# Taking an unread store out of a hybrid-attention kernel and giving two projections other PSUM banks

## Chip, core and metric

The kernel runs on one core of one Trainium2 chip. The metric is device time in microseconds (us) of one execution; smaller is better. The change is judged against the median of three runs of the kernel before.

## What is computed

One decoder block on a sequence of 1024 tokens with 1024 channels: a normalisation, one wide input projection, native sparse attention beside an RWKV-7 recurrence, a gated merge, and a convolutional feed-forward network. Only the first part of it is touched by the change:

```python
h = _rms_norm(x, norm_mix[l])
u = h @ w_in[l]
q, kc, vc, ks, vs, kw, vw, nsa_gl, rw, merge = _split(u, IN_SPLITS)
# in the attention:
qh    = _rms_norm(q.reshape(B, S, G, HG, Dh), qk_gain[0])   # four pairs of heads
k_slc = _rms_norm(ks ..., qk_gain[2])                       # "selected" keys
k_win = _rms_norm(kw ..., qk_gain[3])                       # "local" (window) keys
```

The normalised input `h` is used by every column of `u`, and nowhere else.

## The kernel before, in words

The data lie transposed: 8 chunks of 128 channels, each with 1024 tokens, cut into two halves of 512 tokens (`H[0]`, `H[1]`). Products are made exact enough by splitting each operand into a high part (`hhi`, `whi`) and a rest (`hlo`, `wlo`): `mm3` issues 24 matmuls for one output of 128 by 512, first eight times (hi times hi, lo times hi), then eight times hi times `wlo`.

**Normalisation.** For each half, ScalarE squares the eight chunks, TensorE sums them (L291), ScalarE makes `rstd`. Then `normed` goes through the eight chunks: VectorE writes `hf` (L205), a DMA of the SyncE queue stores it to `h_d` (L207), ScalarE copies it to `hhi` (L208), and VectorE, or GpSimd for chunks 1, 4 and 7 (`NPOOL`), writes `hlo` (L209). `hf` has three buffers, so the fourth chunk writes over the first one's. `hprep`, which would read `h_d`, is in no list of work.

**First projections.** `kphase` projects compressed keys and values (`W01`, banks P and B), adds a position term on VectorE (L349, tile `zpe`, which needs the load `pe`), runs 64 small matmuls per matrix (L357), projects the natural-order columns (L393, banks A), and then the selected keys (`"s"`) and local keys (`"w"`) in `project` with the default banks P. Each half of `s`, `w` and of a query pair goes through `rms64` out of its PSUM bank: square on ScalarE (`nsq`, L297), a matmul into a bank M (L299), Ln and Exp on ScalarE (L301, L302), and the product on VectorE that reads the bank for the last time (L303, `kn` or `qn`). `qproj(0)` is the first query pair; the attention itself begins after it.

**Banks.** PSUM has eight banks of 128 by 512, handed out in pairs by tag:

```python
banks = {"P": [0, 1], "M": [2, 3], "A": [4, 5], "B": [6, 7]}
```

In the attention A and B hold scores and outputs, M the maxima and the sums of `rms64`. P also belongs to the fillers: the projections of the recurrence (`zproj`), of the merge gates (`mproj`) and a low-rank stage (`loraproj`, L827), whose twelve outputs per half go through three `zs` buffers to DRAM.

**Order.** Each engine runs its own instructions in a fixed order. That order is made when the program is built: a planner simulates the program with its own costs, takes what is ready, lowest priority number first, and the fillers have numbers 10000 above the attention. All loads and stores are issued by SyncE, in one order. Weights are loaded by `wload` through two buffers of each of `wraw`, `whi` and `wlo`; ScalarE makes `whi` (L218), GpSimd `wlo` (L219).

Of the kernel before, what the change touches and what calls it, by code (L numbers as in the profile page):

```python
# [7 lines left out]
F32 = mybir.dt.float32  # L8
# [9 lines left out]
S = 1024  # L18
# [113 lines left out]
def build(tc, D, dbg=None, upto=99):  # L132
    nc = tc.nc
    V, A, G, T = nc.vector, nc.scalar, nc.gpsimd, nc.tensor
    dbg = dbg or {}

    def load(t, src):
        return nc.sync.dma_start(t, src)

    with ExitStack() as ctx:  # L140
        def pool(name, bufs=1, space=None, stack=ctx, **kw):
            if space is not None:
                kw["space"] = space
            return stack.enter_context(tc.tile_pool(name=name, bufs=bufs, **kw))
# [4 lines left out]
        dr = pool("dram", 1, DRAM)  # L149
# [7 lines left out]
        def P(name, j=0):  # L157
            o = PAR[name][0]
            return par[:, o + j:o + j + 1]
# [16 lines left out]
        def ps(tag):  # L176
            b = banks[tag]
            b.append(b.pop(0))
            return pp.tile([128, 512], F32, name="ps" + tag, tag=f"bank{b[-1]}", bufs=1)
# [5 lines left out]
        hhi, hlo = [None, None], [None, None]  # L185
# [7 lines left out]
        H = [slice(0, 512), slice(512, 1024)]  # L193

        def rstd_of(h, pss, rstd):
            A.activation(rstd[:, H[h]], pss, AF.Ln, bias=epst[:, 0:1], scale=1.0 / 1024)
            A.activation(rstd[:, H[h]], rstd[:, H[h]], AF.Exp, scale=-0.5)

        def ks_(t, k):
            return t[k] if isinstance(t, list) else t[:, k]  # L200

        def normed(h, xs, gname, rstd, hi, lo, tmp, save=None):
            for k in range(8):
                hf = tmp.tile([128, 512], F32, name="hf", bufs=3)
                V.scalar_tensor_tensor(hf, xs[k][:, H[h]], P(gname, k), rstd[:, H[h]], op0=ALU.mult, op1=ALU.mult)  # L205
                if save is not None:
                    nc.sync.dma_start(save[k][:, H[h]], hf)  # L207
                A.activation(ks_(hi[h], k), hf, AF.Copy)  # L208
                (G if k in NPOOL else V).tensor_sub(ks_(lo[h], k), hf, ks_(hi[h], k).bitcast(F32))  # L209

# [2 lines left out]
        def wload(src, nk):  # L213
            hi = wp.tile([128, 8, 128], FR, name="whi", bufs=2)
            lo = wp.tile([128, 8, 128], FR, name="wlo", bufs=2)
            raw = wp.tile([128, 8, 128], F32, name="wraw", bufs=2)[:, :nk]
            lastw[0] = load(raw, src).ins
            A.activation(hi[:, :nk], raw, AF.Copy)  # L218
            G.tensor_sub(lo[:, :nk], raw, hi[:, :nk].bitcast(F32))  # L219
            return hi, lo  # L220

        def mm3(ps, whi, wlo, xhi, xlo, nk):
            n = 0
            for k, a, b in [(k, whi, b) for k in range(nk) for b in (xhi, xlo)] + [(k, wlo, xhi) for k in range(nk)]:
                T.matmul(ps, a[:, k], ks_(b, k), start=(n == 0), stop=(n == 3 * nk - 1))  # L225
                n += 1

        def project(src, xhi, xlo, nk, evac, halves=(0, 1), tag="P"):
            hi, lo = src if isinstance(src, tuple) else wload(src, nk)
            for h in halves:  # L230
                pj = ps(tag)
                mm3(pj, hi, lo, xhi[h], xlo[h], nk)
                evac(h, pj)

        h_d = dr.tile([8, 128, S], F32, name="h_d")
        onsa_d = dr.tile([4, 128, S], F32, name="onsa_d")
        orw_d = [dr.tile([4, 128, 512], F32, name=f"orw_d{h}") for h in range(2)]
        sg_d = dr.tile([16, 128, S], F32, name="sg_d")
# [38 lines left out]
        with ExitStack() as st:  # L277
            xp = pool("x", 1, stack=st)
            W01 = []
            xs = [xp.tile([128, S], F32, name=f"x{k}") for k in range(8)]  # L280
            for h in range(2):
                for k in range(8):
                    load(xs[k][:, H[h]], D["xT"][k][:, H[h]])
                W01.append(wload(D["w_t"][h], 8))
            rstd = xp.tile([128, S], F32, name="rstd")
            for h in range(2):
                pss = ps("M")
                for k in range(8):
                    sq = xp.tile([128, 512], F32, name="sq", bufs=3)
                    A.activation(sq, xs[k][:, H[h]], AF.Square)  # L290
                    T.matmul(pss, ones, sq, start=(k == 0), stop=(k == 7))  # L291
                rstd_of(h, pss, rstd)
                normed(h, xs, "norm_mix", rstd, hhi, hlo, xp, h_d)

        def rms64(px, n, gcol, out, tmp):
            sq = tmp.tile([128, 512], F32, name="nsq", tag="nsq", bufs=2)
            A.activation(sq[:, :n], px, AF.Square)  # L297
            pss = ps(RTAG)
            T.matmul(pss[:, :n], blk, sq[:, :n], start=True, stop=True)  # L299
            rs = tmp.tile([128, 512], F32, name="nrs", bufs=2)  # L300
            A.activation(rs[:, :n], pss[:, :n], AF.Ln, bias=epst[:, 0:1], scale=1.0 / 64)  # L301
            A.activation(rs[:, :n], rs[:, :n], AF.Exp, scale=-0.5)  # L302
            V.scalar_tensor_tensor(out, px, gcol, rs[:, :n], op0=ALU.mult, op1=ALU.mult)  # L303

        WT = D["w_t"]
# [6 lines left out]
        def kstack(nm, br, kh, kl):  # L312
            n = kh.shape[1]
            so = PAR["sel"][0] + br
            for g in range(2):
                own = slice(64 * g, 64 * g + 64)
                oth = slice(64 - 64 * g, 128 - 64 * g)
                nc.sync.dma_start(kst1[nm, g][own], kh[own])
                nc.sync.dma_start(kst1[nm, g][oth], kl[own])
                nc.sync.dma_start(kst2[nm, g][own], kh[own])  # L320
                V.tensor_copy(kst2[nm, g][oth], par[oth, so:so + 1].to_broadcast([64, n]))

        def kphase():
            with ExitStack() as st:
                tmp = pool("ktmp", 1, stack=st)
# [16 lines left out]
                for kv in range(2):  # L342
# [4 lines left out]
                    def ev(h, pj):  # L347
                        for j in range(2):
                            V.tensor_tensor(z[:, j, 32 * h:32 * h + 32], pj.rearrange("p (n l) -> p n l", l=16),  # L349
                                            pe[:, kv, 16 * j:16 * j + 16][:, None, :].to_broadcast([128, 32, 16]),  # L350
                                            op=ALU.add)
# [53 lines left out]
                for nm, br, wi, gi in (("s", 0, 2, 2), ("w", 1, 3, 3)):  # L405
                    kh = tmp.tile([128, S], F16, name="kh")
                    kl = tmp.tile([128, S], F16, name="kl")

                    def ev(h, pj):
                        kn = tmp.tile([128, 512], F32, name="kn", bufs=2)  # L410
                        rms64(pj, 512, P("gain", gi), kn, tmp)
                        A.activation(kh[:, H[h]], kn, AF.Copy)
                        V.tensor_sub(kl[:, H[h]], kn, kh[:, H[h]])

                    project(WT[wi], hhi, hlo, 8, ev)
                    kstack(nm, br, kh, kl)
                    yield KY[2 + br]

# [3 lines left out]
        qpair = {}  # L422
        mark = {}

        def qproj(i):
            qh = AQ["p"].tile([128, S], F16, name="qh", bufs=2)
            ql = AQ["p"].tile([128, S], F16, name="ql", bufs=2)

            def ev(h, pj):
                qn = AQ["p"].tile([128, 512], F32, name="qn", tag="nsq", bufs=2)  # L430
                rms64(pj, 512, P("gain", 0), qn, AQ["p"])
                if 'qn' in dbg:
                    nc.sync.dma_start(dbg['qn'][i][:, H[h]], qn)
                A.activation(qh[:, H[h]], qn, AF.Copy)
                V.tensor_sub(ql[:, H[h]], qn, qh[:, H[h]])

            project(WT[4 + i], hhi, hlo, 8, ev)
            qpair[i] = (qh, ql)

        def attention():  # L440
            yield from kphase()
            AQ["p"] = pool("attq", 1, stack=ast)
            for i in range(2):
                m = AQ["p"].tile([128, 8, 64], F16, name=f"Mt{i}")
                G.memset(m, 0.0)
                Mt.append(m)
            qproj(0)
            yield KY[4]
            for i in range(4):
                qh, ql = qpair.pop(i)  # L450
# [157 lines left out]
        def reload(src):  # L608
            hi, lo = ktiles(FP["h"], "hhi"), ktiles(FP["h"], "hlo")
            for k in range(8):  # L610
                t = FP["f"].tile([128, 512], F32, name="zs", bufs=NZS)
                load(t, src(k))
                A.activation(hi[k], t, AF.Copy)
                V.tensor_sub(lo[k], t, hi[k].bitcast(F32))
            return hi, lo

        def hprep(h):
            hhi[h], hlo[h] = reload(lambda k: h_d[k][:, H[h]])

        def nsaprep():  # L620
            nsa["hi"], nsa["lo"] = reload(lambda k: onsa_d[k % 4][:, H[k // 4]])
# [605 lines left out]
        with ExitStack() as st:  # L1227
            tp_ = pool("rt", 1, stack=st)
            rstd = tp_.tile([128, S], F32, name="rstd")
# [23 lines left out]
        for g0 in range(0, 22, GR):  # L1253
            ks = range(g0, min(22, g0 + GR))
            hd_, wd_ = [], []
            for i in ks:
                uv = []
                for o in range(2):
                    ci = 22 * o + i
                    hi, lo = wload(D["f_up"][ci], 8)  # L1260
# [71 lines left out]
```

## Time and profile before

| | us |
|---|---|
| median of three runs (lowest, highest) | 1910.56 (1908.12, 1914.51) |
| the profiled execution | 1910.36 |
| its span, first to last instruction | 1908.6 |
| TensorE (PE) busy in the span | 1838.6 |
| VectorE (DVE) busy | 974.3 |
| mean granted TensorE clock (1 is full speed) | 0.98 |

In the rows of the profile PE is TensorE's matmuls, PEld its weight loads, DVE VectorE, ACT ScalarE, POOL GpSimd and SPq SyncE's queue of DMA issues; L205 is line 205 of the kernel. A row of a timeline gives the start and the duration in us, the engine, line and operation, out<-in, and in brackets how long the engine was idle before it and what ended that.

### The profile page before, as it was taken

Reading aid. Unit: us, or ns where it says so; the run is one execution under the profiler, and the core shown is the slowest. Engines: PE = TensorE matmul, PEld = TensorE weight load, DVE = VectorE, ACT = ScalarE, POOL = GpSimd, SP = SyncE. Lnnn points to the kernel's source line nnn. Section 1 sums busy time; section 2 is a strip of 40 time slices with the busy share of each in tenths; the row PEclk is TensorE's granted clock in tenths of the full one; section 3 lists DMA queues with packets and bytes.
Section 4 is the critical chain, followed back from the end, with each engine's and each line's share of the span. In section 5 each row is a group of like instructions: output and inputs, shape, how many; then the busy total and the mean of one; then the engine's idle time right before and its main releaser. Section 6 shows DMA issues by size and latency. Waiting matters only on the chain.

```text
span 1908.6 us, 30508 instructions
## 1 busy us (share of the span) xinstructions
PE 1838.6 (96%) x12106; PEld 1421.8 (74%) x12106; DVE 974.3 (51%) x1775; ACT 794.4 (42%) x1432; POOL 655.6 (34%) x412
## 2 busy tenths in 40 slices
PE   7999999999999999999999799999999999999998
PEld 4876557676767778778777578778888888888886
DVE  4313556777676411984444444355566653444444
ACT  4333565656655632455555443344222222222220
POOL 4312123122333334211245444756444433213220
PEclk9999899999999999899999899999999999999999
DMA  7414234132333435354553454426222211111102
GB/s 247 133 39 144 73 116 133 49 120 62 108 130 115 143 124 201 127 167 156 173 176 118 154 160 141 164 93 215 83 88 78 89 61 56 44 34 58 42 12 88
DMA packets 123647, 215.42 MB, mean 113 GB/s; under 512 B 23921, under 2 KB 52977, under 8 KB 123249
## 3 DMA queue, kind: packets, MB, share of 16 engines
q1 hardware_dynamic: 123504, 213.48, 33.9%
q8 instruction: 95, 1.56, 0.3%
q14 instruction: 48, 0.39, 0.1%
HBM read 151.00 MB, written 57.67 MB: 109 GB/s over the span
## 4 chain that ended last, share of the span: by engine, by line
PE 44%; DVE 2%; DMA 2%; issue 2%; ACT 1%; POOL 0%; SPq 0%; POOLq 0%; ACTq 0%
PE psA L225 11%; PE psP L225 9%; PE psM L225 9%; PE psP L1307 6%; PE psB L1307 6%; DMA s<-sg_d 1%; DVE hf L205 1%; PE psA L1084 1%; PE psM L1003 0%; DVE fu L723 0%; DMA draw<-f_dn 0%; DMA zs<-orw_d 0%; PE psC L1137 0%; DVE yl L677 0%; PE psC L1142 0%
## 5 line engine op out<-in xcount | busy, mean ns | idle before, releaser
L219 POOL TENSOR_TENSOR wlo<-wraw,whi 128x1024 fp32r<-128x1024 f32 (+1 forms) x154 | 346.5, 2251 | 589.2 <-ACT whi L218 174.8
L225 PE MATMUL psP<-hhi,whi 128*128 128x512 f32 x848 | 350.4, 414 | 22.8 <-ACT hhi L708 8.1
L225 PE MATMUL psP<-hlo,whi 128*128 128x512 f32 x848 | 345.7, 408 | 3.6 <-DVE hlo L709 2.4
L218 ACT ACTIVATE whi<-wraw 128x1024 fp32r<-128x1024 f32 (+1 forms) x154 | 152.4, 990 | 222.6 <-PE psP L225 97.9
L225 PE MATMUL psP<-hhi,wlo 128*128 128x512 f32 x848 | 224.6, 399 | 0.0
L225 PEld LDWEIGHTS psP<-hhi,whi 128*128 128x128 f32 x848 | 164.4, 194 | 65.5 <-ACT hhi L708 9.9
L225 PEld LDWEIGHTS psP<-hlo,whi 128*128 128x128 f32 x848 | 164.3, 194 | 42.7 <-DVE hlo L709 3.7
L225 PEld LDWEIGHTS psP<-hhi,wlo 128*128 128x128 f32 x848 | 158.2, 189 | 35.1 <-issue 1.2
L542 DVE TENSOR_TENSOR pl<-pf,ph 128x512 f16<-128x512 f32 (+4 forms) x208 | 122.8, 598 | 45.5 <-ACT pf L541 44.7
L540 ACT ACTIVATE ph<-psA 128x512 f16<-128x512 f32 (+4 forms) x208 | 98.8, 475 | 84.2 <-PE psA L535 60.7
L484 DVE TENSOR_REDUCE mp<-psM 128x1 f32<-128x512 f32 (+1 forms) x192 | 94.1, 515 | 47.6 <-PE psM L482 39.4
L1294 POOL TENSOR_TENSOR dl<-draw,dh 128x1024 fp32r<-128x1024 f32 x22 | 53.2, 2434 | 156.1 <-ACT dh L1293 96.9
L541 ACT ACTIVATE pf<-psA 128x512 f32<-128x512 f32 (+4 forms) x208 | 99.3, 477 | 0.0
L1271 DVE SCALAR_TENSOR_TENSOR u<-psA,par,u 128x511 f32<-128x511 f32 x64 | 47.7, 746 | 100.8 <-ACT u L1267 100.4
L1309 DVE TENSOR_TENSOR x<-x,psP 128x512 f32<-128x512 f32 x88 | 60.3, 685 | 69.1 <-PE psP L1307 68.7
L1293 ACT ACTIVATE dh<-draw 128x1024 fp32r<-128x1024 f32 x22 | 22.3, 1053 | 152.4 <-PE psB L1307 148.2
L1309 DVE TENSOR_TENSOR x<-x,psB 128x512 f32<-128x512 f32 x88 | 60.3, 685 | 45.2 <-PE psB L1307 45.2
L1271 DVE SCALAR_TENSOR_TENSOR u<-psM,par,u 128x511 f32<-128x511 f32 x64 | 47.8, 746 | 64.8 <-ACT u L1267 64.4
L1288 POOL TENSOR_TENSOR hl<-th,hh 128x1024 fp32r<-128x1024 f32 x22 | 52.9, 2402 | 74.6 <-ACT hh L1287 74.6
L545 PEld LDWEIGHTS <-ph 128*128 128x128 f16 (+1 forms) x592 | 55.8, 96 | 23.5 <-issue 10.8
L550 PEld LDWEIGHTS <-pl 128*128 128x128 f16 (+1 forms) x592 | 55.2, 98 | 22.5 <-DVE pl L542 7.9
L1307 PE MATMUL psP<-hh,dh 128*128 128x512 f32 x176 | 69.0, 392 | 2.1 <-ACT hh L1287 2.1
(374 smaller groups left out, 4204.7 us busy)
## 6 DMA issues: line engine op xcount, KB each, us to landing
wraw<-f_up SPq DMA_DIRECT2D x68, 512.0 KB, 3.3
wraw<-w_t SPq DMA_DIRECT2D x46, 512.0 KB, 3.6
draw<-f_dn SPq DMA_DIRECT2D x22, 512.0 KB, 3.2
sg_d<-zs SPq DMA_DIRECT2D x32, 256.0 KB, 2.0
wraw<-w_out SPq DMA_DIRECT2D x16, 512.0 KB, 3.4
z_d<-zs SPq DMA_DIRECT2D x28, 256.0 KB, 2.2
x<-xT SPq DMA_DIRECT2D x24, 256.0 KB, 5.9
zs<-sg_d SPq DMA_DIRECT2D x24, 256.0 KB, 3.0
```

The source lines that it names most:

```text
L218: A.activation(hi[:, :nk], raw, AF.Copy)
L219: G.tensor_sub(lo[:, :nk], raw, hi[:, :nk].bitcast(F32))
L225: T.matmul(ps, a[:, k], ks_(b, k), start=(n == 0), stop=(n == 3 * nk - 1))
L484: V.reduce_max(mp[:, x, br, t:t + 1], pm[:, 0:(b1 - b0) * 128], axis=AX.X)
L540: A.activation(ph[0:nkey, rg], pa[0:nkey, rg], AF.Exp, scale=0.125)
L541: A.activation(pf[0:nkey, rg], pa[0:nkey, rg], AF.Exp, scale=0.125)
L542: V.tensor_sub(pl[0:nkey, rg], pf[0:nkey, rg], ph[0:nkey, rg])
L545: T.matmul(pov[:, t, :], ph[0:nkey, tk], vt[0:nkey, kb, g, 0:65], start=first, stop=False, skip_group_check=True)
L550: T.matmul(pov[:, t, :], pl[0:nkey, tk], vt[0:nkey, kb, g, 0:65], start=False, stop=True, skip_group_check=True)
L1271: V.scalar_tensor_tensor(u[:, e0 + d:e0 + 512], pj[:, 0:512 - d], cw_, u[:, e0 + d:e0 + 512], op0=ALU.mult, op1=ALU.add)
L1307: T.matmul(pj, a[:, m], b[:, H[h]], start=(n == 0), stop=(n == 3 * len(hd_) - 1))
L1309: V.tensor_add(x2[m][:, H[h]], x2[m][:, H[h]], pj)
```

## The change

The store of `hf` to `h_d`, the tensor `h_d`, and the function that would have read it are gone. The local keys' projection writes banks B in place of P, and that of the first query pair banks A in place of P. The other query pairs stay in P.

```diff
-        def normed(h, xs, gname, rstd, hi, lo, tmp, save=None):
+        def normed(h, xs, gname, rstd, hi, lo, tmp):
             for k in range(8):
                 hf = tmp.tile([128, 512], F32, name="hf", bufs=3)
                 V.scalar_tensor_tensor(hf, xs[k][:, H[h]], P(gname, k), rstd[:, H[h]], op0=ALU.mult, op1=ALU.mult)
-                if save is not None:
-                    nc.sync.dma_start(save[k][:, H[h]], hf)
                 A.activation(ks_(hi[h], k), hf, AF.Copy)
...
-        h_d = dr.tile([8, 128, S], F32, name="h_d")
...
-                normed(h, xs, "norm_mix", rstd, hhi, hlo, xp, h_d)
+                normed(h, xs, "norm_mix", rstd, hhi, hlo, xp)
...
-                    project(WT[wi], hhi, hlo, 8, ev)
+                    project(WT[wi], hhi, hlo, 8, ev, tag="PB"[br])
...
-        def qproj(i):
+        def qproj(i, tag="P"):
...
-            project(WT[4 + i], hhi, hlo, 8, ev)
+            project(WT[4 + i], hhi, hlo, 8, ev, tag=tag)
...
-            qproj(0)
+            qproj(0, "A")
...
-        def hprep(h):
-            hhi[h], hlo[h] = reload(lambda k: h_d[k][:, H[h]])
```

`br` is 0 for the selected keys (banks P as before) and 1 for the local keys (banks B).

## Rows read from the trace of the kernel before

**Rows 1.** The page: the span, the busy time of each engine (us, share of the span, instructions), and the granted TensorE clock in 40 slices of 47.7 us, in tenths.
```profile
span 1908.6 us, 30508 instructions
PE 1838.6 (96%) x12106; PEld 1421.8 (74%) x12106; DVE 974.3 (51%) x1775; ACT 794.4 (42%) x1432; POOL 655.6 (34%) x412
PEclk9999899999999999899999899999999999999999
```

**Rows 2.** The page: the chain of work that ended last, by engine.
```profile
PE 44%; DVE 2%; DMA 2%; issue 2%; ACT 1%; POOL 0%; SPq 0%; POOLq 0%; ACTq 0%
```

**Rows 3.** Stretches of the span (from and to, us): length, then busy us (instructions) of PE, PEld, DVE, ACT and POOL, then the granted TensorE clock, the DMA share and GB/s.
```profile
20.00:30.00 10.00, 8.36 (x29) 4.96 (x28) 5.10 (x7) 5.59 (x10) 5.33 (x3) 1.00 0.55 155
30.00:40.00 10.00, 5.70 (x16) 4.13 (x15) 2.88 (x5) 1.26 (x2) 1.28 (x1) 0.69 0.81 281
...
55.47:126.68 71.21, 71.21 (x455) 63.46 (x453) 16.31 (x38) 19.34 (x47) 14.77 (x6) 1.00 0.29 88
...
130.00:140.00 10.00, 8.07 (x25) 5.34 (x24) 1.05 (x2) 4.11 (x7) 3.38 (x5) 0.84 0.42 95
...
180.00:190.00 10.00, 7.85 (x26) 2.65 (x25) 4.27 (x10) 2.52 (x4) 3.66 (x6) 0.87 0.74 235
190.00:200.00 10.00, 10.00 (x25) 3.28 (x25) 2.47 (x5) 3.25 (x5) 2.00 (x3) 0.50 0.48 184
200.00:210.00 10.00, 10.00 (x40) 5.89 (x39) 1.03 (x5) 2.59 (x5) 2.15 (x4) 0.77 0.38 134
```

**Rows 4.** What DVE waited for between 17 and 56 us: us in total, times, longest.
```profile
DVE hf L205 <- DMA h_d<-hf: 11.6, 6, 4.0
...
DVE zpe L349 <- DMA pe<-pe: 3.8, 1, 3.8
DVE hlo L209 <- ACT hhi L208: 1.6, 2, 0.9
```

**Rows 5.** The lines of `normed` between 17.6 and 55.4 us, each from the view of its own line: count, duration in ns (least, median, most), first and last start; the last row is the landing of the 16 stores.
```profile
L205 DVE SCALAR_TENSOR_TENSOR hf<-x,par,rstd x16: 737/748/1489, 17.6 to 48.4; 128x512 f32<-128x512 f32 x16
...
L209 DVE TENSOR_TENSOR hlo<-hf,hhi x10: 678/686/983, 19.7 to 49.0; 128x512 fp32r<-128x512 f32 x10
L209 POOL TENSOR_TENSOR hlo<-hf,hhi x6: 1277/1470/1671, 20.3 to 49.9; 128x512 fp32r<-128x512 f32 x6
...
DMA to landing us min/median/max: 2.0/2.8/7.4
```

**Rows 6.** Timelines of DVE and of POOL, in the first normalisation and, from 1282 us on, in the second one, which stores nothing.
```profile
17.65 2.08 DVE L205 SCALAR_TENSOR_TENSOR hf<-x,par,rstd 128x512 f32<-128x512 f32 x3 [9.40 <-ACT rstd L197]
22.28 2.39 POOL L219 TENSOR_TENSOR wlo<-wraw,whi 128x1024 fp32r<-128x1024 f32 x1 [0.71 <-ACT whi L218]
...
41.38 1.67 POOL L209 TENSOR_TENSOR hlo<-hf,hhi 128x512 fp32r<-128x512 f32 x1 [4.38 <-ACT hhi L208]
42.11 1.49 DVE L205 SCALAR_TENSOR_TENSOR hf<-x,par,rstd 128x512 f32<-128x512 f32 x1 [0.22 <-DMA h_d<-hf]
...
49.87 1.29 POOL L209 TENSOR_TENSOR hlo<-hf,hhi 128x512 fp32r<-128x512 f32 x1 [2.59 <-ACT hhi L208]
...
1282.89 2.76 POOL L219 TENSOR_TENSOR wlo<-wraw,whi 128x1024 fp32r<-128x1024 f32 x1 [3.23 <-ACT whi L218]
1283.32 2.88 DVE L205 SCALAR_TENSOR_TENSOR hf<-x,par,rstd 128x512 f32<-128x512 f32 x1
```

**Rows 7.** Timeline of PE from the first to the last matmul of the projections of compressed keys and values, and the first one after them (55.47, the selected keys).
```profile
20.46 0.80 PE L225 MATMUL psP<-hhi,whi 128*128 128x512 f32 x1
21.56 1.02 PE L291 MATMUL psM<-sq,ones 128*128 128x512 f32 x2
...
51.21 0.51 PE L225 MATMUL psP<-hlo,whi 128*128 128x512 f32 x1 [0.23 <-POOL hlo L209]
...
53.65 1.98 PE L225 MATMUL psB<-hhi,wlo 128*128 128x512 f32 x8
55.47 0.40 PE L225 MATMUL psP<-hhi,whi 128*128 128x512 f32 x1
```

**Rows 8.** Timeline of SyncE's queue.
```profile
31.73 17.74 SPq L207 DMA_DIRECT2D h_d<-hf  x11
51.72 0.33 SPq L138 DMA_DIRECT2D pe<-pe  x1
```

**Rows 9.** Timeline of PE after the second half of the local keys, in the first query pair and at the first filler (139.26).
```profile
128.44 0.50 PE L225 MATMUL psP<-hhi,whi 128*128 128x512 f32 x1 [1.76 <-DVE kn L303]
...
129.47 0.61 PE L225 MATMUL psP<-hhi,whi 128*128 128x512 f32 x1
...
132.87 0.41 PE L225 MATMUL psP<-hhi,whi 128*128 128x512 f32 x1
...
138.70 1.12 PE L299 MATMUL psM<-nsq,cst_f 128*128 128x512 f32 x2 [1.93 <-ACT nsq L297]
139.26 0.99 PE L225 MATMUL psP<-hhi,whi 128*128 128x512 f32 x1
...
143.03 0.44 PE L225 MATMUL psP<-hhi,whi 128*128 128x512 f32 x1
```

**Rows 10.** The low-rank stage's matmuls in its first half (170 to 215 us), as in rows 5.
```profile
L827 PE MATMUL psP<-zwa,lora x16: 589/876/1220, 177.0 to 200.2; 64*128 64x512 f32 x16
L827 PE MATMUL psP<-zg,lora x8: 592/1059/1220, 179.8 to 202.2; 128*128 128x512 f32 x8
```

## The prediction

> **What bounds the kernel.** I read the page first. TensorE is busy for 1838.6 us of a span of 1908.6 [rows 1], and it leads the chain that ended last with 44%, while no other engine or the DMAs have more than 2% [rows 2]. So a microsecond counts where TensorE stands still, or where it runs at half its clock, and anything else is cover. Then I went through the span in stretches of 10 us, looking for PE below 10 or a clock below 1.00. In the part that the change touches there are two such places: 20 to 40 us, where PE is busy 8.36 and 5.70 and the clock falls to 0.69, and around 130 us with 8.07 and 0.84 [rows 3]. Between them, from 55.47 to 126.68 us, PE is busy throughout at clock 1.00, so what is won in the first place is carried on into the second.
>
> The first place is the normalisation. VectorE's waits name the cause: `hf` waited 11.6 us in six waits for the DMA that stores it [rows 4]. With three buffers the fourth `hf` cannot be written before the first store has landed. A store takes 2.8 us to land, at most 7.4 [rows 5], and the last eleven of the 16 leave SyncE's one queue from 31.73 us on, over 17.74 us [rows 8]. TensorE eats each `hlo` as it comes: the last of them, by POOL from 49.87 for 1.29 [rows 6], releases the matmul at 51.21, and 4.26 us later, at 55.47, the selected keys begin [rows 7].
>
> The second place is the pair of banks P. TensorE stops for 1.76 us until `kn` has read its bank, and for 1.93 us before the second sum of the first query pair [rows 9].
>
> **Part 1: the store goes.** Removed are 16 issues on SyncE and 16 waits for landings; no engine's work is removed, and none is added. What is then late next is VectorE's and GpSimd's own work, and the question is whether the two overlap. Three `hf` in a row take 2.08, so 0.69 each [rows 6], and a subtraction on VectorE 0.68 [rows 5]: 16 x 0.69 + 10 x 0.68 = 17.8 us. GpSimd has six subtractions at its undisturbed 1.28 [rows 5] and one `wlo` of 2.39 [rows 6]: 10.1 us. Where they meet, they do not overlap. The `hf` at 42.11 began while a GpSimd subtraction ran until 43.05 and ended at 43.60, 0.55 after it, instead of taking 0.69 from its start; the one at 1283.32 took 2.88 beside a `wlo` that ended at 1285.65 and ended 0.55 after that [rows 6]. The other side waits too: the subtraction at 41.38 took 1.67 against 1.28.
>
> The Trainium skill has a rule for this (SBUF — State Buffer, section Who interferes with whom): a VectorE instruction with two inputs in SBUF and a GpSimd instruction that reads SBUF share one pair of ports, and the one that starts first holds it for its whole length. By that rule the two engines' sums add up; without it the longer one alone would count. The rows of both normalisations agree with the rule.
>
> So the chain is serial: 17.8 + 10.1 = 27.9 us from 17.65, which puts the last `hlo` at 45.6. ScalarE's copies lie beside it, but the 1.6 us that VectorE waits for `hhi` now [rows 4] may stay, and gives 47.2 at the latest; handovers overlap by the 0.1 or so that 0.55 is shorter than 0.69. I take the middle, 46.3. The last `hlo` now lands at 49.87 + 1.29 = 51.16, so this part gives 4.9 us. What follows the last `hlo` stays 4.26 us: 18 matmuls. The load `pe`, which now leaves at 51.72 after the last store [rows 8] because its tile lies where the normalisation's lay, moves with the last `hlo` too; its wait of 3.8 on VectorE [rows 4] stays behind TensorE's tail.
>
> The bounds: if the engines overlapped after all, VectorE would be through at about 37 to 39, and TensorE's own work would set the end. From 20.46 it has 96 matmuls (two column groups, two halves, 24 each) at (55.47 - 53.65) / 8 = 0.228, with two rows of 1.02 for squares [rows 7]: 23.9 us of the 35.0 it takes now, a gain of 11.1 at most. The lower end is 2: the ring of three `hf` then waits for GpSimd's subtraction, queued behind `wlo`, as often as for the stores. The gaps that stay (some 0.8 us a chunk) are shorter than the one before the fall at 30 to 40, where the clock read 0.69 [rows 3]; at 20 to 30, with gaps that sum to 1.64, it read 1.00. So I add no clock loss.
>
> **Part 2: other banks.** Nothing is removed or added: 24 matmuls a half stay 24. The local keys in B find banks that the compressed values left long ago; the first query pair in A finds them after the last natural-order tile. No bank P is then held through a `rms64` chain after the selected keys, so the first `zproj` can start while the chain of the first query pair runs. What can go is the 1.76 and the 1.93, and the slow clock behind each: eight matmuls from 129.47 to 132.87 took 3.40 where eight at 0.228 take 1.82, and eight from 139.26 to 143.03 took 3.77 [rows 9]: 1.58 and 1.95. Sum 7.2 us. The low end is nothing: the planner makes a new order, and PE can stop at the sum of squares (the matmul at 138.70) wherever that is put too early. The 1.76 is a bank wait and must go; for the other a filler has to be put in. Nearer to the upper end, I take 6. The attention starts no earlier than its `qd` copies allow, but its cover, `zproj`, is ready, since the weights follow the same two buffers as now.
>
> **Sum.** 1910.4 (the profiled execution, 0.2 below the median) - 4.9 - 6.0 = 1899.5 us. All later work moves forward with it; 0.3% (5.7 us) is about what this measurement can tell from no change.
>
> **The rivals.**
> 1. The engines overlap in the normalisation and TensorE's work sets the end: -11.1 - 6.0 gives 1893.3. For it: VectorE is idle for 11.6 us on stores alone; against it: rows 6.
> 2. The banks only move the stall: -4.9 alone, 1905.5. For it: the wait at 138.70 is for ScalarE's square, not for a bank [rows 9].
> 3. The store was not what held the chain: GpSimd's subtractions hold the ring as long. About -1 and -6: 1903.4. Against it: six waits end at a store's landing [rows 4].
> 4. Slower: the fillers now run ahead of the attention and meet the low-rank stage alone. Its first half takes 26 us for 24 matmuls [rows 10], paced by three `zs` buffers and their stores, and attention matmuls fill it. At 1.18 a pair (two at the least 0.59) its own work is 14.2, so uncovered it loses 12 us, both halves 24. Today's episode there already costs 2.15 idle and (0.13 + 0.50 + 0.23) x 10 = 8.6 of clock [rows 3], 10.8 in all. Net +13; with the fillers spent, part 2 gives nothing, and a further fall of the clock as long as today's adds up to 8.6: 1910.4 - 4.9 + 13 to 21.6, about 1922. It decides from 10.8 us of loss on (1905.5 to 1916.3, 0.3% above the median), when both halves run without attention beside them.
> 5. Same: the new order makes one more episode like that of 180 to 210: 1899.5 + 10.8 = 1910.
>
> **How the numbers follow.** Chances: forecast 0.46, rival 1 0.13, rival 2 0.15, rival 3 0.08, rival 4 0.08, rival 5 0.10. The forecast and rival 1 are faster by over 0.3% (below 1904.8); rivals 2 and 3 lie at that line, and I count 0.13 of their 0.23 as faster. Faster 0.72, same 0.20, slower 0.08. The range leaves out rivals 4 and 5 (0.18): it reaches from 1890, a little under the upper ends of both parts (11.1 and 7.2, 1892.1), to 1909, a little over their low ends (2 and 0, 1908.4).
>
> **What would show it.** No row for the store; VectorE's waits in the normalisation on ScalarE or none, with `hf` rows of 1.2 to 1.5 beside GpSimd; the last `hlo` at 46 and the selected keys at about 50.5. Around 120 us PE goes from the local keys through both halves of the query pair into `zproj` without a wait above 0.5, at clock 1.00, some 5 us earlier than now and then 11. Wrong: last `hlo` at 39 (rival 1), a new wait at L299 (rival 2), or a clock below 0.9 at a place where it is 1.00 now (rivals 4 and 5).

## The result and the profile after

The changed kernel takes 1890.78 us (median of four executions, 1888.30 to 1894.93) where the kernel before, run beside it, takes 1911.8 (1908.12 to 1914.51): a ratio of 0.9889, with a 95% interval of 0.9869 to 0.9909. That is 21 us, or 1.1%. The forecast was 1899.5 us in a range of 1890 to 1909, and faster: the sign held, and the time came out at the fast end of the range. The profiled execution took 1890.38 us.

The page of the kernel after: span, busy time, granted clock in 40 slices of 47.2 us, and the chain that ended last by engine. They answer to [rows 1, 2].

```profile
span 1888.6 us, 30480 instructions
...
PE 1826.6 (97%) x12106; PEld 1418.5 (75%) x12106; DVE 980.8 (52%) x1775; ACT 797.7 (42%) x1434; POOL 655.6 (35%) x412
...
PEclk9999999999999999899999899999999999999999
...
PE 81%; DVE 8%; DMA 4%; issue 3%; ACT 3%; POOL 1%; SPq 0%; POOLq 0%; DVEq 0%; ACTq 0%
```

TensorE has the same 12106 matmuls and is busy 12.0 us less. The low digit of the clock in the fifth slice of [rows 1], 191 to 239 us, is gone, the two in the middle of the span stay. The chain is followed back over the whole span here (its shares add up to 100, those of [rows 2] to 51), so the 81% is not to be read against the 44%: PE leads it in both.

The code moved up by two to six lines: L207 is now the subtraction that makes `hlo`, L217 the one that makes `wlo`, L223 the projections' matmuls, L296 the sum of squares in `rms64`, L346 `zpe`, L821 the low-rank matmuls.

**The normalisation.** What VectorE waited for between 17 and 56 us (us in total, times, longest), which answers to [rows 4]:

```profile
DVE hf L205 <- ACT rstd L197: 10.0, 1, 10.0
DVE zpe L346 <- PE psA L354: 7.0, 1, 7.0
DVE zpe L346 <- DMA pe<-pe: 3.0, 1, 3.0
```

Four rows of VectorE's timeline, and then three of GpSimd's, which answer to [rows 6]:

```profile
17.48 2.07 DVE L205 SCALAR_TENSOR_TENSOR hf<-x,par,rstd 128x512 f32<-128x512 f32 x3 [9.96 <-ACT rstd L197]
20.29 1.67 DVE L205 SCALAR_TENSOR_TENSOR hf<-x,par,rstd 128x512 f32<-128x512 f32 x1
...
37.52 3.10 DVE L205 SCALAR_TENSOR_TENSOR hf<-x,par,rstd 128x512 f32<-128x512 f32 x3
40.55 1.28 DVE L207 TENSOR_TENSOR hlo<-hf,hhi 128x512 fp32r<-128x512 f32 x2
```

```profile
20.12 1.28 POOL L207 TENSOR_TENSOR hlo<-hf,hhi 128x512 fp32r<-128x512 f32 x1 [3.70 <-ACT hhi L206]
22.11 2.71 POOL L217 TENSOR_TENSOR wlo<-wraw,whi 128x1024 fp32r<-128x1024 f32 x1 [0.70 <-ACT whi L216]
...
41.36 1.61 POOL L207 TENSOR_TENSOR hlo<-hf,hhi 128x512 fp32r<-128x512 f32 x1 [2.62 <-ACT hhi L206]
```

The 11.6 us of waits for the store are gone, and so are the 1.6 us for `hhi`. Between its first `hf` at 17.48 and the end of its last `hlo` at 40.55 + 1.28 = 41.83, no further row of VectorE has an idle time before it: it is either at work or held by GpSimd inside an instruction. The `hf` that starts at 20.29 beside a GpSimd subtraction that runs until 20.12 + 1.28 = 21.40 takes 1.67 and ends 0.56 after it. The last `hlo` is GpSimd's and ends at 41.36 + 1.61 = 42.97, where it ended at 51.16 before.

**What TensorE does with it.** Timeline of PE at the last `hlo` (the matmul at 43.23 takes it) and at the start of the selected keys (47.34), then the end of the first query pair, which now lies in banks A, the first filler (123.74) and a sum of squares (131.34). These answer to [rows 7] and [rows 9].

```profile
42.99 0.39 PE L223 MATMUL psB<-hhi,whi 128*128 128x512 f32 x1
43.23 0.39 PE L223 MATMUL psP<-hlo,whi 128*128 128x512 f32 x1
...
45.52 1.98 PE L223 MATMUL psB<-hhi,wlo 128*128 128x512 f32 x8
47.34 0.40 PE L223 MATMUL psP<-hhi,whi 128*128 128x512 f32 x1
...
121.93 1.98 PE L223 MATMUL psA<-hhi,wlo 128*128 128x512 f32 x8
123.74 0.40 PE L223 MATMUL psP<-hhi,whi 128*128 128x512 f32 x1
...
131.34 1.02 PE L296 MATMUL psM<-nsq,cst_f 128*128 128x512 f32 x2
```

The selected keys begin 8.1 us earlier than at 55.47, and no row from there to the filler has a wait in brackets. The sum of squares, for which PE stopped 1.93 us in [rows 9], now comes at 131.34 between filler matmuls.

The last `hlo` is no longer what TensorE waits for. It ends at 42.97, and the matmul that takes it begins at 43.23, 0.24 after the one before it, like its neighbours. By the profile TensorE's last stop before the selected keys ends at 41.28 (at VectorE's `hlo` that ends at 41.23), and from 20.30 to 47.34 PE is busy for 25.5 of 27.0 us, where before it was for 28.8 of the 35.0 from 20.46 to 55.47, part of it at half clock. So from 41.28 on TensorE's own work sets the end of this place, and 1.6 us at most are left to win there.

**Stretch by stretch.** Stretches of the span (from and to in us, length, busy us and instructions of PE, PEld, DVE, ACT and POOL, granted clock, DMA share, GB/s), of the kernel before:

```profile
0.00:110.00 110.00, 97.60 (x497) 76.09 (x498) 38.67 (x72) 40.61 (x76) 36.12 (x45) 0.97 0.52 165
110.00:160.00 50.00, 46.32 (x202) 35.82 (x201) 10.77 (x22) 17.92 (x31) 8.23 (x7) 0.93 0.28 81
160.00:210.00 50.00, 47.85 (x174) 25.87 (x173) 16.07 (x33) 15.27 (x25) 12.89 (x15) 0.83 0.44 151
```

And of the kernel after:

```profile
0.00:110.00 110.00, 102.14 (x548) 81.29 (x549) 47.02 (x76) 43.56 (x84) 36.83 (x45) 1.00 0.42 127
110.00:160.00 50.00, 50.00 (x219) 39.23 (x218) 12.53 (x22) 22.83 (x35) 11.10 (x8) 1.00 0.40 121
160.00:210.00 50.00, 45.62 (x318) 25.92 (x319) 28.20 (x61) 23.66 (x47) 12.82 (x15) 0.97 0.35 122
```

From 110 to 160 PE is busy throughout at clock 1.00. From 160 to 210 it is busy less than before and yet does 318 matmuls for 174, many of them the attention's shorter ones, at a clock of 0.97 for 0.83. By place of the same work, in the two profiled executions:

| the same work | before | after | lead | won since the row above |
|---|---|---|---|---|
| selected keys, first matmul | 55.47 | 47.34 | 8.1 | 8.1 |
| first filler | 139.26 | 123.74 | 15.5 | 7.4 |
| last low-rank matmul | 288.1 | 266.2 | 21.9 | 6.4 |
| end of the span | 1908.6 | 1888.6 | 20.0 | -1.9 |

The first two rows are the two edits. The third is an episode of slow clock that the sum had not counted as a gain, and the experiments have to say whether it belongs to the change. The kernel before has a second profile, e8 below; against that one the lead at the same four places is 9.4, 17.0, 14.6 and 16.4 us, so there the two edits are worth 17.0 and what lies behind them wins nothing more.

### The profile page after: what moved, and what is told of

Same layout as the page of the kernel before. It is cut to its first block, busy times and chain, and to the rows that moved or that the text cites. A ratio compares the mean times of both kernels' runs of the same rounds, so it can differ in the third digit from the quotient of the medians.

```text
span 1888.6 us, 30480 instructions
## 1 busy us (share of the span) xinstructions
PE 1826.6 (97%) x12106; PEld 1418.5 (75%) x12106; DVE 980.8 (52%) x1775; ACT 797.7 (42%) x1434; POOL 655.6 (35%) x412
## 4 chain that ended last, share of the span: by engine, by line
PE 81%; DVE 8%; DMA 4%; issue 3%; ACT 3%; POOL 1%; SPq 0%; POOLq 0%; DVEq 0%; ACTq 0%
PE psP L223 29%; PE psA L223 12%; PE psM L223 9%; PE psP L1301 6%; PE psB L1301 6%; PE psA L528 1%; PE psA L390 1%; PE psA L530 1%; DVE pl L539 1%; PE psM L997 1%; PE psM L475 1%; DVE mp L481 1%; PE psP L821 1%; DVE hf L205 1%; PE psB L542 1%
## 5 line engine op out<-in xcount | busy, mean ns | idle before, releaser
L217 POOL TENSOR_TENSOR wlo<-wraw,whi 128x1024 fp32r<-128x1024 f32 (+1 forms) x154 | 346.6, 2252 | 577.8 <-ACT whi L216 173.0
L223 PE MATMUL psP<-hhi,whi 128*128 128x512 f32 x816 | 335.2, 412 | 16.5 <-ACT hhi L702 9.9
L223 PE MATMUL psP<-hlo,whi 128*128 128x512 f32 x816 | 330.7, 406 | 3.2 <-DVE hlo L703 1.8
L223 PE MATMUL psP<-hhi,wlo 128*128 128x512 f32 x816 | 215.6, 398 | 0.0
L223 PEld LDWEIGHTS psP<-hhi,whi 128*128 128x128 f32 x816 | 156.8, 193 | 56.2 <-ACT hhi L702 11.9
L223 PEld LDWEIGHTS psP<-hlo,whi 128*128 128x128 f32 x816 | 156.8, 192 | 40.4 <-DVE hlo L703 3.4
L223 PEld LDWEIGHTS psP<-hhi,wlo 128*128 128x128 f32 x816 | 152.5, 190 | 33.6 <-issue 0.7
L1265 DVE SCALAR_TENSOR_TENSOR u<-psA,par,u 128x511 f32<-128x511 f32 x64 | 47.7, 746 | 99.8 <-ACT u L1261 99.4
L1265 DVE SCALAR_TENSOR_TENSOR u<-psM,par,u 128x511 f32<-128x511 f32 x64 | 47.7, 746 | 64.0 <-ACT u L1261 63.7
```

What stands on the lines that cost most here:

```text
L1265: V.scalar_tensor_tensor(u[:, e0 + d:e0 + 512], pj[:, 0:512 - d], cw_, u[:, e0 + d:e0 + 512], op0=ALU.mult, op1=ALU.add)
```

## The experiments

The theory going in was the forecast's: VectorE and GpSimd take turns in the normalisation, the store alone held them up, and the banks are worth the two stalls. The rivals that needed runs: the banks only move the stall; and the third gain is not the change's but the execution's. Each ratio below is to the kernel before, timed on the same chip in the same session.

**e1_store_out: the store alone is taken out**

```diff
-                normed(h, xs, "norm_mix", rstd, hhi, hlo, xp, h_d)
+                normed(h, xs, "norm_mix", rstd, hhi, hlo, xp)
```

> The store alone is taken out; the local keys and the first query pair stay in banks P. Theory A (the store holds the ring of hf, the banks hold the query chain, each for itself): the selected keys begin at 47.3 us as in the changed kernel (55.5 before), the two waits of 1.8 and 1.9 us after the local keys are back with the slow clock behind them, and the time is 8 us under the kernel before, some 1903 to 1904. Theory B (the earlier start also moves the low-rank stage to a better place, and that is worth the 6 us that neither part accounts for): 14 us under it, 1897. Theory C (the 4 MB of stores slow the loads and the rest): the time goes down, but VectorE's waits in the normalisation don't all go.

Measured: 1898.61 us against 1913.4, ratio 0.9921 (0.9897 to 0.9945). The selected keys begin at 47.75. What PE waited for from 45 to 160 us:

```profile
PE psM L299 <- ACT nsq L297: 3.2, 2, 1.9
PE psP L225 <- DVE kn L303: 1.8, 1, 1.8
```

Of the first gain 7.7 us are there without the banks, and the two stops of [rows 9] are still there, 8 us earlier, with a third of 1.28 us between them (at 127.69; the second profile of the kernel before, e8, has it too, 1.29 at 136.64). The time does not follow theory A: it is 14.8 us under the kernel before, where theory A says 8 and theory B 14. So the places account for about half of what e1 wins. Its stretch from 160 to 210 us has a granted clock of 0.97.

**e2_banks: the banks alone are changed**

```diff
-                    project(WT[wi], hhi, hlo, 8, ev)
+                    project(WT[wi], hhi, hlo, 8, ev, tag="PB"[br])
...
-            qproj(0)
+            qproj(0, "A")
```

> The banks alone are changed; the store stays. Theory A: the selected keys begin at 55.5 us as before, PE runs from the local keys through the query pair into the first filler with no wait, the filler begins at 132 instead of 139.3, and the time is 7.4 us under the kernel before, some 1904. Theory B' (it is the fillers' head start from free banks P that puts the low-rank stage in a better place): 14 us under it, 1897. If the banks only move the stall: no change.

Measured: 1901.68 us against 1913.4, ratio 0.9943 (0.9922 to 0.9963). The selected keys begin at 56.04 and the first filler at 132.53, 76.49 us later; before it is 139.26 - 55.47 = 83.79, in the changed kernel 123.74 - 47.34 = 76.40. So the banks are worth 7.3 to 7.4 us, with the store or without it, and rival 2 (the banks only move the stall) does not hold for the two edits together. The time is 11.7 us under the kernel before, between theory A (7.4) and theory B (14): here too some 4 us are not in these places. The stretch from 110 to 160 us:

```profile
110.00:160.00 50.00, 50.00 (x246) 41.28 (x246) 12.75 (x22) 21.45 (x37) 11.04 (x8) 1.00 0.32 91
```

PE does 246 matmuls there for 202 before, with no wait at all.

**e3_store_out_local: e1, and the local keys alone in B**

```diff
-                    project(WT[wi], hhi, hlo, 8, ev)
+                    project(WT[wi], hhi, hlo, 8, ev, tag="PB"[br])
```

> Store out, local keys in B, the first query pair still in P. Theory A: the wait of 1.8 us for kn goes, since the query pair finds P free; the first filler then waits for the query pair's chain to read P, some 2 us and a slow clock of 2 us, so 4 us over the changed kernel, 1895. If the local keys' bank is what counts: as the changed kernel, 1891.

Measured: 1906.03 us, ratio 0.9959 (0.9940 to 0.9978); the expectation was missed by 11 us, and the median is 7 us above that of e1, of which this kernel is an extension. What PE waited for longest from 45 to 330 us, and two stretches:

```profile
PE psM L299 <- ACT nsq L297: 5.3, 2, 3.3
```

```profile
110.00:160.00 50.00, 44.75 (x180) 32.99 (x179) 10.04 (x19) 17.11 (x27) 9.04 (x8) 0.90 0.33 94
160.00:210.00 50.00, 47.62 (x194) 25.94 (x192) 16.37 (x34) 16.70 (x28) 12.13 (x15) 0.83 0.40 137
```

The wait for `kn` has gone, as it must, but the query pair now comes sooner to its own sum of squares and has nothing else to run there: 5.3 us of stops where e1 has 5.0. This is the forecast's rival 2, true of this half of the edit. By itself it costs little more than e1: from the first matmul of the selected keys (47.67) to the one behind the last of those stops (131.57) it is 83.90 us, against 130.74 - 47.75 = 82.99 in e1. Most of the rest of the miss lies in 160 to 210, where a clock of 0.83 takes 0.17 x 50 = 8.5 us. Of the twelve executions four lie from 1898.65 to 1901.09, as fast as e1, and eight from 1904.60 to 1911.91; the profiled one, 1911.40, is the second slowest.

**e4_store_out_q0: e1, and the first query pair alone in A**

```diff
-            qproj(0)
+            qproj(0, "A")
```

> Store out, first query pair in A, local keys still in P. Theory A: the query pair doesn't wait for kn, and by the time the first filler wants a bank P the local keys' chains have read both, so nothing waits: as the changed kernel, 1891 to 1892. If the local keys' bank counts too: 2 to 4 us over it.

Measured: 1895.15 us, ratio 0.9894 (0.9867 to 0.9920), the changed kernel's 0.9889 within its interval. The time itself is 3 us over theory A's 1891 to 1892, where the other theory put it; but it is 18.3 us under the kernel before beside it, and so is the changed kernel in e11 (1892.78 against 1911.03). The places decide. The selected keys begin at 46.85, the first filler at 123.30: 76.45 us. The whole of the second gain is this one edit. With the pair in A, the fillers find both banks P free (the local keys' chains have read them by then) and run through the chain of the pair's `rms64`.

**e5_ring8: the kernel before, with eight buffers for `hf` in place of three**

```diff
-                hf = tmp.tile([128, 512], F32, name="hf", bufs=3)
+                hf = tmp.tile([128, 512], F32, name="hf", bufs=8 if save is not None else 3)
```

> The kernel before, store kept, banks kept, but with eight buffers of hf in place of three, so that the first store to be waited for is that of the ninth chunk. If it is the wait of the ring for a landing that cost the time (and not the 4 MB of traffic, nor the 16 issues): VectorE's waits for the store fall from 11.6 us to under 2, the last hlo lands at about 43 to 44 as without the store, the selected keys begin at 48 to 49 (the load of the position term leaves after the last store), and the time is that of the kernel with the store alone taken out, about 1899. If the traffic or the queue cost it: the selected keys begin at 52 or later.

Measured: 1903.77 us against 1912.05, ratio 0.9964 (0.9944 to 0.9983). What VectorE, TensorE and SyncE's queue waited for, and then rows of VectorE's and the queue's timelines:

```profile
DVE hf L205 <- ACT rstd L197: 10.4, 1, 10.4
DVE zpe L349 <- DMA pe<-pe: 4.7, 1, 4.7
```

```profile
PE psP L225 <- DVE hlo L209: 4.0, 1, 4.0
```

```profile
SPq L138 <- DMA h_d<-hf: 4.7, 4, 2.9
```

```profile
17.89 9.56 DVE L205 SCALAR_TENSOR_TENSOR hf<-x,par,rstd 128x512 f32<-128x512 f32 x8 [10.35 <-ACT rstd L197]
27.38 4.17 DVE L209 TENSOR_TENSOR hlo<-hf,hhi 128x512 fp32r<-128x512 f32 x5
```

```profile
45.89 0.33 SPq L138 DMA_DIRECT2D pe<-pe  x1
```

With more buffers VectorE no longer waits for a store, and its last `hlo` ends at 43.05, as without a store. So it was the landing of the stores through a ring of three, not their issue or their traffic, that cost VectorE its time. But the selected keys begin at 51.78 and not at 48 to 49, almost at the 52 that the other theory names. The rows show another reason for that than traffic: the new order writes eight `hf`, 9.56 us, ahead of the first of VectorE's `hlo` at 27.38, for which TensorE stands still for 4.0 us, its only wait from 17 to 56 us, and from 28 to 32 us the granted clock is 0.50. The loads that reuse the normalisation's memory also wait for the stores to land (4.7 us on SyncE), so `pe` leaves at 45.89 where the changed kernel issues it at 43.00; PE has no wait behind it. The ratio is 0.9964 where taking the store out gives 0.9921 (8.3 us by the medians for 14.8), and the selected keys move by 3.7 us for 7.7: the buffers win about half. (The profile of this kernel, its second slowest execution of ten, also shows a long fall of the clock, 0.86 from 160 to 210; what the late start costs at the end is not told apart from it.)

**e6_no_pool: the changed kernel, with all sixteen `hlo` of the first normalisation on VectorE**

```diff
-                normed(h, xs, "norm_mix", rstd, hhi, hlo, xp)
+                normed(h, xs, "norm_mix", rstd, hhi, hlo, xp, ())
```

(The last argument is the list of chunks that GpSimd subtracts.)

> The changed kernel with all 16 hlo of the first normalisation on VectorE, none on GpSimd. If GpSimd and VectorE exclude one another here: VectorE's 32 operations at 0.69 and 0.68 and one wlo of 2.4 on GpSimd, 24.3 us from 17.5, so the last hlo ends at about 41.8 instead of 43.0, though VectorE has six more operations; the hf rows beside a GpSimd subtraction (1.65) are gone, only the one beside wlo (2.9) stays. If GpSimd's six subtractions were free: VectorE gets 4.1 us longer and the last hlo ends at 47.

Measured, in one execution: 1895.58 us. Timelines of GpSimd and of VectorE:

```profile
22.73 2.48 POOL L217 TENSOR_TENSOR wlo<-wraw,whi 128x1024 fp32r<-128x1024 f32 x1 [6.12 <-ACT whi L216]
```

```profile
23.00 2.75 DVE L205 SCALAR_TENSOR_TENSOR hf<-x,par,rstd 128x512 f32<-128x512 f32 x1
...
26.88 0.74 DVE L205 SCALAR_TENSOR_TENSOR hf<-x,par,rstd 128x512 f32<-128x512 f32 x1
27.55 0.68 DVE L207 TENSOR_TENSOR hlo<-hf,hhi 128x512 fp32r<-128x512 f32 x1
28.15 1.40 DVE L205 SCALAR_TENSOR_TENSOR hf<-x,par,rstd 128x512 f32<-128x512 f32 x2
...
38.93 1.47 DVE L207 TENSOR_TENSOR hlo<-hf,hhi 128x512 fp32r<-128x512 f32 x2
```

VectorE has six instructions more and is through earlier: at 38.93 + 1.47 = 40.40 against 41.83. Had the two engines overlapped, it would have been later by 6 x 0.68 = 4.1. That settles the first half of the forecast's rival 1, that the engines overlap. The one long `hf` left is the one beside `wlo`: 2.75, ending at 25.75, 0.54 after 22.73 + 2.48 = 25.21. The Trainium skill says the same (SBUF — State Buffer, section Who interferes with whom: the ports that the two engines share are an exclusive lock); every `hf` row here agrees with it. The last `hlo` is 2.6 us earlier than the changed kernel's (42.97), but the selected keys begin at 46.30, only 1.0 earlier: TensorE's own work is in the way (PE is busy for 25.2 of the 26.3 us from 20.00 on), the second half of rival 1.

**e7_local_again and e8_before_again: e3 and the kernel before, one more execution each, unchanged**

> The same kernel as e3_store_out_local, profiled a second time. There the clock fell to 0.5 for 18 us in the low-rank stage, after 2.4 us of idle. If the length of that fall belongs to the program's order: again some 18 us, and a span near 1909. If it is a matter of the execution: a fall of 3 to 4 us, and a span near 1900, with the same order of instructions and the same idle before it.

> The kernel before, profiled a second time. The first profile had the clock at 0.5 from 186.5 to 204 us, 8.6 us lost. If the fall belongs to the order of the kernel before: the same again. If to the execution: it may be 3 to 4 us long, and the span some 6 us shorter; then the part of the gain that lies there is no gift of the change.

Measured: 1914.78 us and 1906.78 us. The stretch from 160 to 210 us of e7:

```profile
160.00:210.00 50.00, 45.94 (x190) 25.80 (x190) 17.08 (x34) 16.48 (x27) 12.62 (x15) 0.86 0.39 137
```

The same stretch of e8, and two short ones inside it:

```profile
160.00:210.00 50.00, 47.19 (x200) 28.45 (x200) 18.00 (x37) 18.17 (x31) 12.91 (x15) 0.97 0.46 155
...
184.00:186.00 2.00, 0.70 (x4) 0.29 (x3) 1.52 (x4) 0.06 (x1) 0.62 (x1) 1.00 0.98 383
192.00:194.00 2.00, 2.00 (x11) 0.90 (x10) 1.13 (x3) 1.43 (x3) 0.62 (x1) 1.00 0.51 195
```

The same two short ones in the first profile of the kernel before:

```profile
184.00:186.00 2.00, 0.40 (x3) 0.29 (x2) 0.56 (x2) 0.85 (x2) 0.00 (x0) 1.00 0.71 271
192.00:194.00 2.00, 2.00 (x4) 0.22 (x4) 0.35 (x2) 0.55 (x2) 0.62 (x1) 0.50 0.42 163
```

The same program, with the same instructions in the same order and nearly the same stop at 182 to 187, once runs at half clock from 187.5 to about 204.6 and once only from 187.3 to about 190.8 (read from stretches of 2 us). Its last low-rank matmul starts at 288.1 and at 280.8: 7.3 us, more than the third gain of the table, in a kernel in which nothing was changed. The local keys' kernel had a long fall in both profiles (0.83 and 0.86 from 160 to 210). Against this second profile (span 1905.0) the changed kernel's lead is 16.4 us, near 8.1 + 7.4 = 15.5. Such an execution is not the usual one, as far as a total can tell: of the 59 other executions of the kernel before that the experiments were timed beside, 10 are as fast as its 1906.78.

**e9_zs4 and e10_zs4_no_pool: the changed kernel, and e6, with a fourth buffer `zs`**

```diff
-NZS = 3
+NZS = 4
...
-                                ot = AQ["p"].tile([128, 4, 64], F32, name="ot", bufs=2)
+                                ot = AQ["p"].tile([128, 4, 64], F32, name="ot", bufs=1)
```

(The second line pays for the memory of the first. `NZS` holds for every filler that uses `zs`, not for the low-rank stage alone.)

> The changed kernel with four zs buffers in place of three (and one ot buffer in the attention in place of two, to make room). Theory: the stop in the low-rank stage is the same fault as that of the normalisation, a ring that waits for a store's landing (ScalarE's third output waits 4.4 us for lw_d, everything of ScalarE stands behind it, and TensorE runs out of work). Then ScalarE's waits for lw_d between 150 and 210 us fall from 10.2 us in four to under 3, TensorE's idle between 160 and 180 from 2.7 us to under 1, the clock doesn't fall there, and the time is 3 to 5 us under the changed kernel, some 0.986 to 0.987 of the kernel before. If the stop comes from the attention's own waits: no change.

> As the run before, and all 16 hlo of the first normalisation on VectorE. By the port's rule the selected keys begin 1 us earlier (46.3 as in the run without GpSimd's subtractions, 47.3 with them) and everything after it: 1 us under the run before, which is at the edge of what can be told; if the new order brings a clock fall elsewhere, up to 5 us over it.

**e11_changed_again: the changed kernel, once more beside these two**

> The changed kernel again, beside the two before it on the same chip: 0.989 of the kernel before, and in its profile the same short fall of the clock in the low-rank stage (some 4 us at 0.5, near 170 us). If that fall is a matter of the execution, as in the kernel before, it may be some 18 us long here and the profiled execution 6 us over the others.

Measured, against 1911.03 us for the kernel before in 23 executions: e9 1900.52 (0.9953, 0.9934 to 0.9972), e10 1900.89 (0.9950, 0.9931 to 0.9970), e11 1892.78 (0.9912, 0.9881 to 0.9944). What ScalarE waited for most in the stage, 150 to 210 us, in the changed kernel:

```profile
ACT zs L824 <- DMA lw_d<-zs: 10.2, 4, 4.4
```

In e9, and beside it PE's wait that e9 has anew:

```profile
ACT zs L827 <- DMA lw_d<-zs: 2.4, 1, 2.4
ACT q L502 <- PE psM L500: 5.1, 1, 5.1
```

```profile
PE psM L500 <- DVE Mt L496: 2.8, 1, 2.8
```

The first 20 us of the stage in e9 and then in e11:

```profile
160.00:180.00 20.00, 17.80 (x53) 5.98 (x52) 8.79 (x17) 7.79 (x13) 9.37 (x12) 0.83 0.64 222
```

```profile
160.00:180.00 20.00, 15.82 (x56) 5.50 (x54) 11.26 (x21) 7.06 (x11) 8.44 (x11) 1.00 0.61 210
```

The buffer did what it was meant to do for ScalarE, whose wait for the stores fell from 10.2 to 2.4 us. It did not help: the time is 0.9953 where 0.986 to 0.987 was expected, and PE is idle for 2.2 of the first 20 us where under 1 was. The order is another one, the maxima over compressed keys begin at 191.9 and not at 181.6, and PE stops for 2.8 us at a tile of the attention. Only one buffer of `ot` is another difference, which e9 and e10 share, so the price of each is not told apart. (The profiled execution of e9, 1909.11, is its slowest of twelve.) In e10 the selected keys begin at 45.92, 1.2 us earlier than in e9 (47.13), and nothing of it is left at the end: 1900.89 against 1900.52. The theory that the ring of three `zs` is what brings the slow clock fell. The e11 profile shows the opposite pair: PE stands still for 4.2 us of those 20, more than the 2.2 of e9, at clock 1.00 throughout.

## Why the forecast was right, and where its sizes were off

**The store.** The mechanism held at the points named for VectorE and the queue: no wait of VectorE for a landing, `hf` rows of 1.65 to 1.78 beside a GpSimd subtraction (forecast 1.2 to 1.5), `pe` leaving SyncE with the last `hlo` (43.00 for 51.72), the 18 matmuls behind it unchanged (43.23 to 47.34 is 4.1 us, forecast 4.26). Rival 3, that the store was not what held the chain, fell with e1 and e5. The term was 4.9 and measured 8.1 (7.7 in e1): the last `hlo` ended at 42.97 and not at 46.3. Two steps made most of the difference of 3.3. The chain was taken as the plain sum of the two engines' durations, 27.9 us from the first `hf`; it measured 42.97 - 17.48 = 25.5. And 0.7 was added for about half of ScalarE's 1.6 us of waits, which disappeared wholly. The rows show where most of the 2.4 comes from. The last GpSimd subtraction begins at 41.36 while VectorE runs until 41.83, and still ends 1.14 after it instead of 1.28; an `hf` ends 0.56 after GpSimd instead of its own 0.69. That is about 0.27 at each of seven GpSimd instructions, 1.9; the rest may be ends of VectorE's rows that overlap the next start by 0.08 (in e6, 27.55 + 0.68 lies 0.08 beyond 28.15). The forecast named this overlap as "0.1 or so" and did not subtract it.

One thing the forecast had otherwise: what ends the place. It let the last `hlo` decide, with TensorE's own 23.9 us as a far bound. In the changed kernel the two meet: PE is busy for 25.5 of the 27.0 us to the selected keys, and it reaches the last `hlo` without a stop. A shorter chain alone wins little more, as e6 shows (2.6 us for the last `hlo`, 1.0 for the selected keys). So of rival 1 the overlap was false, and TensorE's work at the end was nearly true. Its 1893.3 lies nearer to the measured time than the forecast's 1899.5, but the time did not come about by its overlap.

**The banks.** Forecast 6.0 of an upper end of 7.2; measured 7.3 to 7.4 in the changed kernel, e2 and e4, so both stops went and the slow clock behind each went too. (The parts of the 7.2 vary by execution: e8 has no slow clock behind the 1.76, and a third stop of 1.29 in its place, and takes 140.78 - 56.69 = 84.1 us to the first filler for the first profile's 83.8.) The discount for a stop at the sum of squares was not needed with the pair in A. The forecast gave the two edits one sum; e3 and e4 show that the query pair's bank carries all of it and the local keys' bank none.

**What was not in the sum.** The low-rank stage appears in the forecast only as a possible loss (rivals 4 and 5), and neither came: the fillers did not meet it without attention, since from 160 to 210 PE does 318 matmuls for 174. The forecast's starting point, though, was an execution with the long fall of the clock there. Its 8.6 us were counted in 1910.4 and kept in 1899.5. 1910.4 - 8.1 - 7.4 = 1894.9 would have been the time with the two edits at their measured size. The profiled execution is 4.5 us below that, since its fall in the stage cost 50 x 0.03 = 1.5 us of clock for 50 x 0.17 = 8.5, and 1.9 of what the stage won was given back later. So of the 9.1 us between the forecast and the profiled execution 3.2 are the store's term, 1.4 the banks' and 4.5 the stage's. That the result still lies in the range, 0.8 us above its lower end, is in part luck: that end was put under the full 11.1 and 7.2 of the two parts, and the time came there by another way.

Is that gain the change's? Partly, as far as the runs go. The kernel before shows the short fall too (e8), so part of it is chance. But the two edits alone, at their places, would bring e1 to 1913.4 - 7.7 = 1905.7 and e2 to 1913.4 - 7.4 = 1906.0, and all six executions of e1 and ten of the twelve of e2 are below that; both had a short fall in their profiles. The changed kernel is 21 us under the kernel before in its own runs and 18.3 in e11, where the places give 15.5. That each edit makes the long fall rarer would explain this, and also that the two parts alone add up to more than the whole (0.79% and 0.57% against 1.11%); no run shows it by itself. What decides in an execution whether the clock returns after some 4 us or some 17 stays open: stops of like length were followed by both (e8 and the first profile), and e9, which was meant to settle it, did not.

## What to carry to other kernels

A store that nobody reads takes no time of the engines that compute and can still set the pace: look at what the buffer it reads from must wait for, since through a small ring each landing, 2.0 to 7.4 us here, becomes a wait of the engine that writes the buffer. A result that is held in PSUM through a long chain belongs in banks that the filler work does not use, and one should ask of each projection separately whether anything is ready to fill its chain. And before a profile's time is used as the starting point of a sum, take a second profile of the same kernel: here two executions of one program differed by 7.3 us in one stage.

## What was not expected of the hardware

VectorE and GpSimd exclude one another so strictly that moving six subtractions from GpSimd (1.28 to 1.67 us each) to VectorE (0.68) made VectorE itself finish 1.4 us sooner. And TensorE's clock, after stops of nearly the same length at the same instruction of the same program, stayed at 0.50 for about 17 us in one execution and 3.5 us in another, and in a third, of the changed kernel, 4.2 us of stops within 20 us left it at 1.00.
